# Decoder block on one core: where the down projection's operands are split, and the order of the passes in a granule

## The chip, the cores and the metric

The kernel runs on one core of a Trainium2 chip. The metric is the device time of one execution in microseconds. Three runs of the kernel before took 2098.62, 2100.62 and 2102.5 us (median 2100.62).

## The reference

One decoder block over 512 tokens of width 2048, everything in float32: a token mixer (gated linear attention and differential attention beside each other, from one input projection, joined by one output projection) and a gated MLP with a causal convolution of width 3, each between two RMS norms and added to the residual. Nearly all arithmetic is in four matrix products; the change touches the last one most.

```python
h = rmsnorm(x, attn_pre_norm)
proj = h @ w_in                                   # 512 x 2048 by 2048 x columns of both groups
o = concat(gla(...proj...), diff_attention(...proj...))
x = x + rmsnorm(o @ w_o, attn_post_norm)

h = rmsnorm(x, ffn_pre_norm)
up = h @ w_ffn_in                                 # 2048 x 11264
a, b = up[..., :5632], up[..., 5632:]
a = conv_w[0]*a[t-2] + conv_w[1]*a[t-1] + conv_w[2]*a[t] + conv_b
f = (gelu(a) * b) @ w_ffn_out                     # 5632 x 2048
x = x + rmsnorm(f, ffn_post_norm)
```

## The kernel before

**Three passes for one product.** TensorE multiplies a rounded float32 form. A float32 operand is therefore cut into a high half (the rounded value, a copy on ScalarE) and a low half (the rest, a subtraction on VectorE), and a product is the sum of three passes: high by high, high by low, low by high. `split` (L149 to L151) does this for activations; `granule` (L137, L138) does it for a weight tile of 128 x 1024, called a granule. The halves of the weights lie in one tensor `ring` with three places for high and three for low halves; in the down stage every fourth granule goes to a pair of spare tiles, `xhi` and `xlo`. Activations lie in `ah` and `al`. So in a row of the profile `ring<-raw,ring` or `ring<-rt,ring` on DVE is the making of a low half, and `bank<-ring,ah` is a pass on either half of the weights.

**Stages.** The projections are computed by a scheme of Winograd's kind: each unit has seven segments (x0, z0, y0, z1, x1, y1, y2) in place of eight block products, of two granules each. The right-hand blocks are sums of weight blocks (made by VectorE, L1212 and L1230, or by loads from the POOL queue that add to the tile in SBUF, L1195 and L1455), the left-hand ones are sums of token blocks, called a11, s5, s2, s3, a12, s7 and a22. In the profiled execution the stages lie about so: start and first projections to 130 us; the mixer's input projection with both attentions woven in to 620; output projection and the way to the MLP, with the first 512 columns of the MLP (`first_pair`, two calls) by plain products, to 880; twenty units of the up projection (ten groups of 512 columns, two branches) to about 1640; ten units of the down projection (five chunks, two halves of the columns) to 2045; the columns of `first_pair` through the down projection (`last_group`, `ffn_out_part`) and the last norm to the end.

**The passes.** `mm_n` (L191 to L193), `InUnit.run` (L742 to L748), `down_prods` (L1349 to L1351) and `ffn_out_part` (L1553 to L1555) issue the three passes of each 128 rows next to each other: high by high, then the one on the weights' low half and the one on the activations' low half. `up_prods` (L1247 to L1249) and `mm_t` (L173 to L175) do so too. A scheduler orders the instructions of each engine within its rules; the change-over from up to down units (`change_over`, `run_in_order`) is in an order written out by hand, with small jobs hung on granules by `at`.

**The down projection's operands.** After the second branch of a group, `product` makes the activations u0 and u1 and `token_sums` stores a11, a12, a22 and, after four sums of 128 x 512 by VectorE (L1322), s5, s2, s7 and s3 to DRAM, 256 KB each, in tensors `sd{c}{name}` (two groups make a chunk c; seven stores a group). The sums use two buffers, tag "sum", in turn. In the down stage `prepare` loads 512 KB of an operand into a tile `st` and splits it: ScalarE writes `ah` (L150), VectorE writes `al` (L151), 35 times in all. In the change-over five of these are cut into a load and a split, hung on different granules, and the last group's four sums are hung on four granules. `first_pair` stores its activations in `ud0`, which the last stage loads and splits in the same way, twice.

## Time and profile before

| | |
|---|---|
| runs, median | 2100.62 us |
| profiled execution | 2097.49 us |
| its span | 2095.8 us |
| split of a weight granule: ScalarE, VectorE | 1.06 us, 1.22 us |
| sum of 128 x 512 on VectorE (L1322) | 0.68 us |
| operand loads `st<-sd..`, 512 KB | 35, median 3.2 to 8.2 us to landing, by tensor |
| operand stores `sd..<-u` and `sd..<-s`, 256 KB | 70, median 2.1 to 6.5 us to landing, by tensor |

The profile is of one execution, on the hardware's own clock. The span runs from the first to the last recorded instruction; the execution took 1.7 us more than that. PE is TensorE's matmuls, PEld its weight loads, DVE VectorE, ACT ScalarE, POOL GpSimd, SP the engine that issues most loads and stores. Matmuls are pipelined: their recorded durations overlap, and the spacing of their starts tells the pace. In a list of waits, "bank L1350 <- DVE ring L138" means that the matmul at L1350 stood until VectorE's instruction at L138 had ended. In a row of the timeline the bracket gives the idle time of the engine before the instruction and what ended it.

### The profile page before, as it was taken

The page shows a single profiled execution, that of the slowest core. Times are in us where ns is not written, and L with a number is a line of the kernel's source. Part 1 is how long each engine was busy: PE and PEld are TensorE (multiplying, and loading weights), DVE is VectorE, ACT ScalarE, POOL GpSimd, SP SyncE. Part 2 cuts the span into 40 slices and gives each one's busy share as a digit, 9 for nine tenths or more (in the row PEclk, how much of TensorE's full clock was granted, in tenths as well). Part 3 has the DMA queues.
Part 4 walks back from the last instruction along what each step waited for, and adds up shares of the span by engine and source line. Part 5 has one row for each costly group of instructions (what it writes and reads, how often), then busy time and mean ns, then how long its engine had stood idle before and what let it go on. Part 6 is the DMA issues. An engine that isn't in the chain of part 4 may idle for free.

```text
span 2095.8 us, 35570 instructions
## 1 busy us (share of the span) xinstructions
PE 2059.0 (98%) x14449; PEld 1900.7 (91%) x14449; DVE 1509.7 (72%) x1802; ACT 1002.5 (48%) x1306; POOL 286.3 (14%) x306
## 2 busy tenths in 40 slices
PE   7999999999999999999999999999999999999997
PEld 6699999999988889899999999999999878787786
DVE  5967777676762255976777777777777778888877
ACT  5544444455742233454554554555455554444443
POOL 0112222322200000011011111110111110110100
PEclk9999999999999999999999999999999999999999
DMA  5488887878884344447667577667766876776763
GB/s 210 121 186 182 193 193 177 180 176 196 197 229 151 96 159 151 138 107 192 153 150 192 144 162 186 142 160 173 167 157 181 240 211 166 189 195 159 175 166 141
DMA packets 280696, 358.60 MB, mean 171 GB/s; under 512 B 14592, under 2 KB 221876, under 8 KB 278612
## 3 DMA queue, kind: packets, MB, share of 16 engines
q1 hardware_dynamic: 191380, 259.85, 37.2%
q0 software_dynamic: 84800, 94.38, 29.7%
q8 instruction: 113, 1.85, 0.4%
q10 hardware_dynamic: 4352, 2.10, 0.3%
q14 instruction: 51, 0.42, 0.1%
HBM read 311.72 MB, written 44.56 MB: 170 GB/s over the span
## 4 chain that ended last, share of the span: by engine, by line
PE 60%; issue 30%; DMA 3%; DVE 3%; POOL 3%; ACT 1%; SPq 0%; POOLq 0%; DVEq 0%; ACTq 0%
PE bank L1247 6%; PE bank L1248 6%; PE bank L1249 6%; PE bank L192 3%; PE bank L193 3%; PE bank L191 3%; PE bank L742 3%; PE bank L744 3%; PE bank L743 3%; PE bank L746 3%; PE bank L748 3%; PE bank L747 3%; PE bank L173 2%; PE bank L175 2%; PE bank L174 2%
## 5 line engine op out<-in xcount | busy, mean ns | idle before, releaser
L138 DVE TENSOR_TENSOR ring<-raw,ring 128x1024 fp32r<-128x1024 f32 x315 | 383.4, 1222 | 281.0 <-ACT ring L137 271.1
L137 ACT ACTIVATE ring<-raw 128x1024 fp32r<-128x1024 f32 x315 | 333.2, 1060 | 509.2 <-PE bank L1248 113.9
L1247 PE MATMUL bank<-ah,ring 128*128 128x256 f32 x1280 | 353.4, 276 | 0.0
L1248 PE MATMUL bank<-al,ring 128*128 128x256 f32 x1280 | 353.4, 276 | 0.0
L1249 PE MATMUL bank<-ah,ring 128*128 128x256 f32 x1280 | 353.4, 276 | 0.0
L137 ACT ACTIVATE ring<-rt 128x1024 fp32r<-128x1024 f32 x221 | 233.4, 1060 | 247.8 <-PE bank L1248 154.9
L138 DVE TENSOR_TENSOR ring<-rt,ring 128x1024 fp32r<-128x1024 f32 x221 | 269.1, 1221 | 86.9 <-ACT ring L137 86.7
L1247 PEld LDWEIGHTS bank<-ah,ring 128*128 128x128 f32 x1280 | 240.3, 188 | 0.1
L1248 PEld LDWEIGHTS bank<-al,ring 128*128 128x128 f32 x1280 | 240.3, 188 | 0.1
L1249 PEld LDWEIGHTS bank<-ah,ring 128*128 128x128 f32 x1280 | 240.3, 188 | 0.0
L1350 PE MATMUL bank<-ring,ah 128*128 128x512 f32 x424 | 166.2, 392 | 6.3 <-DVE ring L138 6.3
L1351 PE MATMUL bank<-ring,al 128*128 128x512 f32 x424 | 165.1, 389 | 0.0
L1349 PE MATMUL bank<-ring,ah 128*128 128x512 f32 x424 | 158.3, 391 | 0.0
L192 PE MATMUL bank<-ring,ah 128*128 128x512 f32 x280 | 110.0, 394 | 0.6 <-DVE ring L138 0.6
L191 PE MATMUL bank<-ring,ah 128*128 128x512 f32 x280 | 109.6, 397 | 0.0
L193 PE MATMUL bank<-ring,al 128*128 128x512 f32 x280 | 109.3, 393 | 0.0
L1195 POOL DMA_DIRECT2D raw<-in_w_ffn_in_dram x40 | 51.2, 1309 | 395.5 <-DVE ring L138 395.5
L1350 PEld LDWEIGHTS bank<-ring,ah 128*128 128x128 f32 x424 | 79.6, 188 | 26.1 <-DVE ring L138 9.9
L1349 PEld LDWEIGHTS bank<-ring,ah 128*128 128x128 f32 x424 | 79.5, 188 | 18.1 <-ACT ring L137 1.4
L1195 POOL DMA_DIRECT2D rt<-in_w_ffn_in_dram x40 | 50.9, 1271 | 326.9 <-DVE ring L138 292.4
L1351 PEld LDWEIGHTS bank<-ring,al 128*128 128x128 f32 x424 | 79.6, 188 | 16.3
L746 PE MATMUL bank<-ring,ah 128*128 128x256 f32 x320 | 92.7, 290 | 1.7 <-ACT ring L137 1.0
(346 smaller groups left out, 5670.9 us busy)
## 6 DMA issues: line engine op xcount, KB each, us to landing
raw<-in_w_ffn_in_dram SPq DMA_DIRECT2D x96, 512.0 KB, 5.0
raw<-in_w_in_dram SPq DMA_DIRECT2D x56, 512.0 KB, 4.8
raw<-in_w_ffn_out_dram SPq DMA_DIRECT2D x48, 512.0 KB, 6.2
raw<-in_w_in_dram POOLq DMA_DIRECT2D x40, 512.0 KB, 7.1
rt<-in_w_ffn_in_dram SPq DMA_DIRECT2D x40, 512.0 KB, 5.6
rt<-in_w_ffn_in_dram POOLq DMA_DIRECT2D x40, 512.0 KB, 6.1
raw<-in_w_ffn_in_dram POOLq DMA_DIRECT2D x40, 512.0 KB, 6.8
raw<-in_w_o_dram SPq DMA_DIRECT2D x32, 512.0 KB, 3.9
```

Of the source, the lines that this page charges most:

```text
L137: act(hi, raw, AF.Copy)
L138: tt(lo, raw, hi.bitcast(F32), ALU.subtract)
L191: mm(banks[t], ah[:, t, s, :], w[0][:, k, :], start=st, stop=False)
L192: mm(banks[t], ah[:, t, s, :], w[1][:, k, :], start=False, stop=False)
L193: mm(banks[t], al[:, t, s, :], w[0][:, k, :], start=False, stop=sp)
L746: mm(o, sh[:, n, kk, :], wh[:, k, :], start=st, stop=False, **NOW)
L1247: mm(o, wh, sh[:, :, kk, :], start=start and kk == 0 and n == 0, stop=False, **NOW)
L1248: mm(o, wh, sl[:, :, kk, :], start=False, stop=False, **NOW)
L1249: mm(o, wl, sh[:, :, kk, :], start=False, stop=kk == HK - 1, **NOW)
L1349: mm(b[j], sh[:, o:o + P], w[0][:, q, :], start=start and st == 0, stop=False, **NOW)
L1350: mm(b[j], sh[:, o:o + P], w[1][:, q, :], start=False, stop=False, **NOW)
L1351: mm(b[j], sl[:, o:o + P], w[0][:, q, :], start=False, stop=st == 3, **NOW)
```

## The change

Two things change, and the number of matmuls does not.

First, the operands of the down projection are split where they are made. `store_split` has ScalarE write the high half into a small tile and VectorE write the low half in place, and stores both, 256 KB each, into two tensors (`h` and `l`). `token_sums` now gives eleven jobs: four sums and seven `store_split`s. Sums and high halves share one tag, "t2", of four buffers; s7 is made in the place of a21. `prepare` becomes two loads of 512 KB straight into `al` and `ah`. In the change-over the five loads are hung on other granules, their splits are gone, and the last group's eleven jobs are hung on eleven granules. `first_pair` stores its two parts split as well.

Second, in `mm_n`, `InUnit.run`, `down_prods` and `ffn_out_part` all passes on the weights' high half come first and those on the low half last. `up_prods` and `mm_t` stay.

```diff
     def mm_n(banks, t, g, w, slots=tuple(range(KT))):
-        for k in range(2):
+        for v, p, k in ((ah, 0, 0), (al, 0, 0), (ah, 0, 1), (al, 0, 1), (ah, 1, 0), (ah, 1, 1)):
             i = 2 * g + k
-            st, sp, s = i == 0, i == KT - 1, slots[i]
-            mm(banks[t], ah[:, t, s, :], w[0][:, k, :], start=st, stop=False)
-            mm(banks[t], ah[:, t, s, :], w[1][:, k, :], start=False, stop=False)
-            mm(banks[t], al[:, t, s, :], w[0][:, k, :], start=False, stop=sp)
+            mm(banks[t], v[:, t, slots[i], :], w[p][:, k, :], start=i == 0 and p == 0 and v is ah,
+               stop=i == KT - 1 and p == 1)
...
+                for w in (wh, wl):
+                    for n in range(2):
...
+                                mm(o, sh[:, n, kk, :], w[:, k, :], start=st, stop=sp_, **NOW)
+                                if w is wh:
+                                    mm(o, sl[:, n, kk, :], w[:, k, :], start=False, stop=False, **NOW)
...
+    def half_tile(name, dt=F32):
+        return fp.tile([P, 2, 256], dt, name=name, tag="t2", bufs=4)
...
+    def store_split(dst, src, hi):
+        split(hi, src.bitcast(F32R), src)
+        dma(dst(0), hi.bitcast(F32))
+        dma(dst(1), src)
...
-        dma(ud0[:, 2 * pr:2 * pr + 2, :], c)
+        store_split(lambda v: ud0[v][:, 2 * pr:2 * pr + 2, :], c, small_tile("hi", F32R).rearrange("p (n t) -> p n t", n=2))
...
-        def put(n, src):
-            dma(sd[c][n][:, i, :].rearrange("p (n t) -> p n t", n=2), src)
-
-        def add(n, x, y, op):
+        def add(n, x, y, op, dst=None):
             def go():
-                t = made[n] = fp.tile([P, 2, 256], F32, name=n, tag="sum", bufs=2)
-                tt(t, made.get(x, x) if isinstance(x, str) else x, y, op)
-                put(n, t)
+                made[n] = half_tile(n) if dst is None else dst
+                tt(made[n], made.get(x, x) if isinstance(x, str) else x, y, op)
             return go
 
-        put("a11", a11)
-        put("a12", a12)
-        put("a22", a22)
-        return (add("s5", a21, a22, ALU.subtract), add("s2", "s5", a11, ALU.subtract),
-                add("s7", a11, a21, ALU.subtract), add("s3", "s2", a12, ALU.add))
+        def out(n, src=None):
+            def go():
+                store_split(lambda v: sd[c][n][v][:, i, :].rearrange("p (n t) -> p n t", n=2),
+                            made[n] if src is None else src, half_tile("hi", F32R))
+            return go
+
+        return (add("s5", a21, a22, ALU.subtract), add("s7", a11, a21, ALU.subtract, a21),
+                add("s2", "s5", a11, ALU.subtract), out("s5"), add("s3", "s2", a12, ALU.add), out("s2"),
+                out("s3"), out("a11", a11), out("s7"), out("a12", a12), out("a22", a22))
...
     def prepare(c, n):
-        raw = small_tile("st")
-        dma(raw, sd[c][n].rearrange("p g x -> p (g x)"))
-        split(piece(ah, *place[n]), piece(al, *place[n]), raw)
+        for v, d in zip((ah, al), sd[c][n]):
+            dma(piece(v, *place[n]).bitcast(F32), d.rearrange("p g x -> p (g x)"))
 
     def down_prods(b, op, g, w, start):
         sh, sl = (piece(v, *place[op]) for v in (ah, al))
-        for j in range(2):
-            for q in range(2):
-                o = 512 * g + 256 * q + P * j
-                st = 2 * g + q
-                mm(b[j], sh[:, o:o + P], w[0][:, q, :], start=start and st == 0, stop=False, **NOW)
-                mm(b[j], sh[:, o:o + P], w[1][:, q, :], start=False, stop=False, **NOW)
-                mm(b[j], sl[:, o:o + P], w[0][:, q, :], start=False, stop=st == 3, **NOW)
+        for p in range(2):
+            for j in range(2):
+                for q in range(2):
+                    o = 512 * g + 256 * q + P * j
+                    st = 2 * g + q
+                    mm(b[j], sh[:, o:o + P], w[p][:, q, :], start=start and st == 0 and p == 0,
+                       stop=st == 3 and p == 1, **NOW)
+                    if p == 0:
+                        mm(b[j], sl[:, o:o + P], w[0][:, q, :], start=False, stop=False, **NOW)
...
-        prepare_at(0, "s2", (u, "x1", 0), (u, "y1", 0))
-        prepare_at(0, "s3", (u, "x1", 1), (d0, "x0", 0))
-        prepare_at(0, "s7", (u, "y1", 1), (u, "y2", 0))
-        prepare_at(0, "a12", (d0, "x0", 0), (d0, "z0", 0))
-        prepare_at(0, "a22", (u, "y2", 0), (d0, "y0", 0))
+        at(u, "x1", 1, lambda: prepare(0, "s2"))
+        at(u, "x1", 1, lambda: prepare(0, "s3"))
+        at(u, "y1", 1, lambda: prepare(0, "s7"))
+        at(u, "y1", 1, lambda: prepare(0, "a12"))
+        at(u, "y2", 1, lambda: prepare(0, "a22"))
...
-        for where in ((d0, "z0", 0), (d0, "y0", 0), (d0, "z1", 0), (d0, "x1", 0)):
+        spread = [(d0, seg, g) for seg in ("z0", "y0", "z1", "x1", "y1") for g in range(2)] + [(d1, "x0", 0)]
+        for where in spread:
             at(*where, lambda: late_sums.pop(0)())
...
+        for v, p, k in [(v, 0, k) for k in range(4) for v in range(2)] + [(0, 1, k) for k in range(4)]:
+            mm(b, us[k][v][:, tk], gr[k // 2][p][:, k % 2, :], start=(v, p, k) == (0, 0, 0),
+               stop=(p, k) == (1, 3))
```

What stands on the engines now, at three places (numbers behind a name tell buffers apart).

PE in a down unit, one granule into two banks; of the passes on `ring,ah` before the change, L1349 is on the high half of the weights and L1350 on the low half. Before (each bank's first L1349 stands a few rows ahead of these):

```order
L1350 MATMUL bank_17768<-ring_84,ah_79 128x512
L1351 MATMUL bank_17768<-ring_84,al_80 128x512
L1349 MATMUL bank_17768<-ring_84,ah_79 128x512
L1350 MATMUL bank_17768<-ring_84,ah_79 128x512
L1351 MATMUL bank_17768<-ring_84,al_80 128x512
L1350 MATMUL bank_17769<-ring_84,ah_79 128x512
L1351 MATMUL bank_17769<-ring_84,al_80 128x512
L1349 MATMUL bank_17769<-ring_84,ah_79 128x512
L1350 MATMUL bank_17769<-ring_84,ah_79 128x512
L1351 MATMUL bank_17769<-ring_84,al_80 128x512
```

After, where L1357 is the pass on `ah` with either half, and the rows with x2 at the end of each granule are on the low half:

```order
L1357 MATMUL bank_17548<-ring_84,ah_79 128x512
L1360 MATMUL bank_17548<-ring_84,al_80 128x512
L1357 MATMUL bank_17548<-ring_84,ah_79 128x512
L1360 MATMUL bank_17548<-ring_84,al_80 128x512
L1357 MATMUL bank_17549<-ring_84,ah_79 128x512
L1360 MATMUL bank_17549<-ring_84,al_80 128x512
L1357 MATMUL bank_17549<-ring_84,ah_79 128x512
L1360 MATMUL bank_17549<-ring_84,al_80 128x512
L1357 MATMUL bank_17548<-ring_84,ah_79 128x512 x2
L1357 MATMUL bank_17549<-ring_84,ah_79 128x512 x2
```

Eight passes on the high half stand ahead of the four on the low half, where one on each half alternated.

VectorE in the up stage, after the product of the first group (`u_9365` and `u_9192` before, `u_9180` and `u_9235` after, hold its activations; L1230 and L1239 add weight blocks; L138 makes low halves of weights). Before:

```order
L1322 TENSOR_TENSOR s5_9539<-u_9365,u_9192 128x512
L138 TENSOR_TENSOR ring_84<-rt_9425,ring_84 128x1024
L1322 TENSOR_TENSOR s2_9542<-s5_9539,u_9365 128x512
L138 TENSOR_TENSOR ring_84<-raw_9608,ring_84 128x1024
L1230 TENSOR_TENSOR rt_9425<-rt_9425,raw_9724 128x1024
L1322 TENSOR_TENSOR s7_9545<-u_9365 128x512
L138 TENSOR_TENSOR ring_84<-raw_9610,ring_84 128x1024
L138 TENSOR_TENSOR ring_84<-raw_9722,ring_84 128x1024
L1322 TENSOR_TENSOR s3_9548<-s2_9542,u_9192 128x512
L138 TENSOR_TENSOR ring_84<-raw_9724,ring_84 128x1024
L1275 TENSOR_TENSOR u_9606<-bank_9553,u_9606 128x2x256
```

After, with the four sums at L1327 and the low halves of the operands at L151; first from the sum s5 on:

```order
L1327 TENSOR_TENSOR s5_9578<-u_9180,u_9235 128x512
L138 TENSOR_TENSOR ring_84<-rt_9467,ring_84 128x1024
L1327 TENSOR_TENSOR u_9180<-u_9180 128x2x256
L1327 TENSOR_TENSOR s2_9581<-s5_9578,u_9180 128x512
L138 TENSOR_TENSOR ring_84<-raw_9677,ring_84 128x1024
L1239 TENSOR_TENSOR rt_9467<-rt_9467,raw_9793 128x1024
L151 TENSOR_TENSOR s5_9578<-s5_9578,hi_9583 128x512
L1327 TENSOR_TENSOR s3_9588<-s2_9581,u_9235 128x512
L138 TENSOR_TENSOR ring_84<-raw_9679,ring_84 128x1024
L138 TENSOR_TENSOR ring_84<-raw_9791,ring_84 128x1024
```

and from there to the last of the seven splits:

```order
L151 TENSOR_TENSOR s2_9581<-s2_9581,hi_9590 128x512
L151 TENSOR_TENSOR s3_9588<-s3_9588,hi_9595 128x512
L138 TENSOR_TENSOR ring_84<-raw_9793,ring_84 128x1024
L151 TENSOR_TENSOR u_9180<-u_9180,hi_9600 128x2x256
L1284 TENSOR_TENSOR u_9675<-bank_9622,u_9675 128x2x256
L138 TENSOR_TENSOR ring_84<-raw_9677,ring_84 128x1024
L151 TENSOR_TENSOR u_9180<-u_9180,hi_9605 128x2x256
L138 TENSOR_TENSOR ring_84<-raw_9679,ring_84 128x1024
L151 TENSOR_TENSOR u_9235<-u_9235,hi_9610 128x2x256
L151 TENSOR_TENSOR u_9235<-u_9235,hi_9615 128x2x256
```

The four sums stand close together, and seven splits of half size have come in among the low halves of the weights.

ScalarE at the same place, after the change; each `hi` is a tile of tag "t2":

```order
L150 ACTIVATE hi_9583<-s5_9578 128x512
L137 ACTIVATE ring_84<-raw_9679 128x1024
L137 ACTIVATE ring_84<-raw_9791 128x1024
L150 ACTIVATE hi_9590<-s2_9581 128x512
L1282 ACTIVATE u_9675<-bank_9469 128x2x256
L150 ACTIVATE hi_9595<-s3_9588 128x512
L137 ACTIVATE ring_84<-raw_9793 128x1024
L150 ACTIVATE hi_9600<-u_9180 128x512
L137 ACTIVATE ring_84<-raw_9677 128x1024
L150 ACTIVATE hi_9605<-u_9180 128x512
L137 ACTIVATE ring_84<-raw_9679 128x1024
L150 ACTIVATE hi_9610<-u_9235 128x512
```

Before, the rows between L1271 and the next L1085 were weight splits and one L1273 alone.

SyncE, which issues loads and stores in this order, where the second chunk's operands are loaded. Before:

```order
L48 DMA st_17404<-sd1a11_8335 128x1024
L48 DMA st_17440<-sd1s5_8338 128x1024
L48 DMA sd4s2_8360<-s2_17090 128x512
L48 DMA sd4s7_8361<-s7_17120 128x512
L48 DMA st_17480<-sd1s2_8339 128x1024
L102 DMA raw_17300<-in_w_ffn_out_dram 128x2x512
L102 DMA raw_17302<-in_w_ffn_out_dram 128x2x512
L102 DMA raw_17368<-in_w_ffn_out_dram 128x2x512
L102 DMA raw_17370<-in_w_ffn_out_dram 128x2x512
L48 DMA sd4s3_8362<-s3_17160 128x512
```

After:

```order
L48 DMA al_80<-sd1s5l_8350 128x1024
L48 DMA ah_79<-sd1s5h_8349 128x1024
L102 DMA raw_17824<-in_w_ffn_out_dram 128x2x512
L48 DMA al_80<-sd1s2l_8352 128x1024
L48 DMA ah_79<-sd1s2h_8351 128x1024
L102 DMA raw_17826<-in_w_ffn_out_dram 128x2x512
L102 DMA raw_17896<-in_w_ffn_out_dram 128x2x512
L48 DMA al_80<-sd1s3l_8356 128x1024
L48 DMA ah_79<-sd1s3h_8355 128x1024
L102 DMA raw_17898<-in_w_ffn_out_dram 128x2x512
L48 DMA al_80<-sd1a12l_8346 128x1024
L48 DMA ah_79<-sd1a12h_8345 128x1024
```

An operand was one row (`st`) and is now two, `al` and `ah`.

66 lines of the change are left out of this document (22 added, 44 removed).

## The prediction

> **What bounds the kernel now.** I read the page first: the engines' shares, the slices, the chain that ended last.
>
> ```profile
> PE 2059.0 (98%) x14449; PEld 1900.7 (91%) x14449; DVE 1509.7 (72%) x1802; ACT 1002.5 (48%) x1306; POOL 286.3 (14%) x306
> ...
> PE   7999999999999999999999999999999999999997
> ...
> PE 60%; issue 30%; DMA 3%; DVE 3%; POOL 3%; ACT 1%; SPq 0%; POOLq 0%; DVEq 0%; ACTq 0%
> ```
>
> PE sets the time: it is busy in every slice but the two ends, and the chain is PE and its issue. The change leaves the number of matmuls alone, so it can only fill PE's gaps or open new ones. Where the gaps lie comes from the windows (columns: stretch and length, then busy us and instructions of PE, PEld, DVE, ACT, POOL; then PE clock, DMA share, GB/s).
>
> ```profile
> 130.00:620.00 490.00, 484.63 (x3934) 470.58 (x3933) 344.68 (x576) 257.20 (x426) 109.90 (x124) 1.00 0.83 189
> ...
> 850.00:900.00 50.00, 50.00 (x287) 43.92 (x286) 46.38 (x44) 23.41 (x26) 2.57 (x2) 1.00 0.34 85
> 880.00:1630.00 750.00, 750.00 (x6596) 749.11 (x6595) 563.97 (x554) 385.18 (x438) 100.77 (x79) 1.00 0.69 162
> 1630.00:1700.00 70.00, 67.35 (x364) 56.64 (x363) 53.20 (x53) 35.74 (x41) 7.15 (x6) 1.00 0.84 245
> 1700.00:2045.00 345.00, 339.68 (x1487) 277.89 (x1486) 286.65 (x306) 157.43 (x160) 40.19 (x34) 1.00 0.68 176
> 1750.00:1800.00 50.00, 50.00 (x222) 41.44 (x221) 41.27 (x46) 23.74 (x24) 5.33 (x6) 1.00 0.74 194
> 1800.00:1850.00 50.00, 48.47 (x213) 39.50 (x212) 40.43 (x44) 19.77 (x20) 6.49 (x6) 1.00 0.76 183
> ```
>
> The up stage (880 to 1630) has no gap at all; the stretch 1800 to 1850 has nine matmuls fewer than its neighbour, whose 222 in 50 us give the undisturbed spacing, 0.225 us for 512 columns. (In the up stage 6596 in 750 us give 0.114 us for 256 columns.) So the down stage and the hand-ordered change-over ahead of it lose time, the up stage does not. What PE waits for there comes from its list of waits (waited for: us in total, times, longest).
>
> ```profile
> PE bank L158 <- DVE xt L247: 10.4, 2, 9.5
> PE bank L1350 <- DVE ring L138: 6.3, 8, 1.0
> PE bank L1350 <- DVE xlo L138: 1.6, 3, 0.8
> ...
> PE bank L746 <- ACT ring L137: 1.0, 1, 1.0
> PE bank L175 <- DVE xlo L138: 0.8, 1, 0.8
> PE bank L1554 <- DVE xlo L138: 0.8, 1, 0.8
> PE bank L748 <- DVE ring L138: 0.8, 1, 0.8
> ...
> PE bank L192 <- DVE ring L138: 0.6, 1, 0.6
> ```
>
> Every wait of the down stage is at L1350, the matmul on the weights' low half, and is for DVE's L138, which makes that half. The first row (start) and L746 (high half) are not touched. The costliest of the L1350 waits, PE first, then DVE ahead of it, then ACT:
>
> ```profile
> 1820.59 0.62 PE L1349 MATMUL bank<-ring,ah 128*128 128x512 f32 x2
> 1822.24 0.50 PE L1350 MATMUL bank<-ring,ah 128*128 128x512 f32 x1 [1.03 <-DVE ring L138]
> ```
>
> ```profile
> 1818.70 1.22 DVE L1230 TENSOR_TENSOR rt<-rt,raw 128x1024 f32<-128x1024 f32 x1
> 1819.84 1.22 DVE L151 TENSOR_TENSOR al<-st,ah 128x1024 fp32r<-128x1024 f32 x1
> 1820.97 1.22 DVE L138 TENSOR_TENSOR ring<-rt,ring 128x1024 fp32r<-128x1024 f32 x1
> ```
>
> ```profile
> 1812.88 1.06 ACT L137 ACTIVATE xhi<-rt 128x1024 fp32r<-128x1024 f32 x1 [4.60 <-DMA rt<-in_w_ffn_out_dram]
> ```
>
> An accumulating load landed late, ACT had stood for 4.60 us, DVE worked off the backlog, and the operand's own split (L151) stood right in front of the low half that PE needed. Both parts of the change act here.
>
> **Gain: the late low halves.** Two matmuls began at 1820.59, the second some 0.23 us later, at 1820.82; the next at 1822.24. That is 1.42 us for a spacing of 0.23, so the wait cost 1.19 where the record says 1.03: 0.16 more, the drained pipe. The 11 waits of L1350 (6.3 + 1.6 = 7.9 us) then cost 7.9 + 11 x 0.16 = 9.7 us; L1554, L748 and L192, one each, (0.8 + 0.8 + 0.6) + 3 x 0.16 = 2.7 us. L175 is in a function that the change leaves as it is. Together 12.4 us can go.
>
> Do they go? With the passes reordered, eight matmuls of a down granule lie ahead of the first one on the low half, where one or two did: six more at least, 6 x 0.225 = 1.35 us. The longest wait, 1.19, is inside that. L748 gets 14 to 15 more of 0.114 (1.6 us), L1554 as much as L1350, L192 three of 0.225 (0.7 us, for a wait of 0.76). The 35 splits that leave the down stage come on top. Their rows, and those of what replaces them (columns: busy us, mean ns):
>
> ```profile
> L151 DVE TENSOR_TENSOR al<-st,ah 128x1024 fp32r<-128x1024 f32 x35 | 42.6, 1217 | 0.0
> ...
> L150 ACT ACTIVATE ah<-st 128x1024 fp32r<-128x1024 f32 x34 | 35.8, 1052 | 9.7 <-PE bank L1350 8.6 <-DMA st<-ud 0.9
> ```
>
> ```profile
> L137 ACT ACTIVATE ring<-rt 128x1024 fp32r<-128x1024 f32 x157 | 167.0, 1064 | 182.2 <-PE bank L1248 150.8 <-issue 9.4 <-DMA raw<-in_w_ffn_in_dram 6.6
> ...
> L1271 ACT ACTIVATE u<-bank 128x512 f32<-128x512 f32 x20 | 11.6, 580 | 0.0
> ```
>
> ```profile
> L1322 DVE TENSOR_TENSOR s<-s,u x20: 683/688/694, 973.2 to 1679.7; 128x512 f32<-128x512 f32 x20
> ```
>
> 42.6 us leave DVE (busy 286.65 of 345 there) and 35.8 leave ACT. As neither is the bound on average, this saves nothing beyond the same waits.
>
> **Cost 1: the splits in the up stage.** Each of ten groups gets seven half-size splits: 7 x 0.69 = 4.8 us of DVE and 7 x 0.58 = 4.1 us of ACT; nine groups lie in the up stage. DVE has room there on average (563.97 of 750), but in the rows of the new order the group fills DVE: from the first sum to the last half-size split stand seven low halves and one weight add (8 x 1.22), four sums, seven splits and one addition of a bank (12 x 0.69), 18 us while PE goes through seven granules, 19 us. A granule has slack: 24 matmuls of 0.114 are 2.7 us; with three ring slots a slot falls free two granules (5.4 us) before PE needs its new contents, of which ACT's 1.06 and DVE's 1.22 use 2.3. So 3.1 us of delay are hidden at each granule. What could use them up are the stores: the new split writes into one of four small tiles, and a tile is free only once its store has landed. Before, DVE waited so:
>
> ```profile
> DVE s L1322 <- DMA sd1s<-s: 6.1, 2, 3.7
> ```
>
> ```profile
> DMA to landing us min/median/max: 2.0/4.8/5.9
> ```
>
> (The second row is for the eight stores of tile sd1s.) The reuses form chains of three links (a tile is written by ACT, stored, written again), with about two weight splits, 5.4 us of PE's time, in a link. A split and a store of the median length, 0.58 + 4.8, just fit. Bounds: 0, or 2.5 us for each of nine groups, 22 us, if the delays add up; I take 1.5 us in all, near the lower end, because before the change a wait of 3.7 us on DVE cost PE nothing in this stage.
>
> **Cost 2: the first pairs.** Two full-size splits, 2 x 1.22 us of DVE, join the stretch 850 to 900, where DVE has 46.38 of 50 us. It can't hide all: 0 to 2.5 us, taken 1.5.
>
> **Cost 3: the change-over.** Five split steps leave it, seven half-size ones with fourteen stores come in, in a stretch with a DMA share of 0.84. It loses 2.65 us now (70.00 - 67.35). I let 2.0 us of that stand or come back; bounds 0 and 5.
>
> **Cost 4: the traffic.** An operand now arrives as two halves of the full size.
>
> ```profile
> q1 hardware_dynamic: 191380, 259.85, 37.2%
> q0 software_dynamic: 84800, 94.38, 29.7%
> ...
> rt<-in_w_ffn_out_dram POOLq DMA_DIRECT2D x20, 512.0 KB, 8.5
> ...
> sd1a<-u SPq DMA_DIRECT2D x6, 256.0 KB, 6.5
> ```
>
> The hardware queue moved 259.85 MB in 0.372 x 2095.8 = 780 us of 16 engines, 3.0 us each MB. 35 more loads of 0.52 MB are 18.4 MB, 55 us over some 400 us of down stage: its share goes from 0.68 to about 0.82. The loads sit on SP's queue among the weights, in units with an even number, where they may push an accumulating load (8.5 us already) later. Bounds: 0, or 1.2 us in each of five such units, 6 us; taken 1.0, since the new lead of 1.35 us takes most of it.
>
> **Sum.** -12.4 + 1.5 + 1.5 + 2.0 + 1.0 = -6.4 us. The profiled execution took 2097.49 us (its span 2095.8, 1.7 around it), which becomes 2091.1; the median of the runs shown is 2100.62, 3.1 above that execution. On the median's scale the forecast is 2100.6 - 6.4 = **2094.2 us**.
>
> **A rule of the skill against the change.** The row of sd1a stands for three stores issued close together: 6.5 us each, where a lone 256 KB store took 2.0. The Trainium skill, DMA: Bandwidth & Descriptors, "Rules for kernel authors", says to coalesce small transfers into large ones and to aim at 1 MiB; the change does the reverse, with two stores of 256 KB where one was. That rule would have the bunch of fourteen decide: it is the first rival below. The same page, "Queues, rings and completion order", says that an engine takes turns between queues packet by packet; by that a store beside one accumulating load would take about twice its 2.0 us, 4 us, and the first rival would not come to pass. The measured median of 4.8 and maximum of 5.9 lie between the two, nearer the first.
>
> **Rivals.**
>
> 1. *ACT waits for stores in the up stage (slower).* A link with a store of sd1a's length takes 0.58 + 6.5 = 7.1 us instead of 5.4; three links put ACT 5.1 us behind, 2.0 more than the hidden 3.1. It decides from a landing time of 5.9 us (3 x 1.07 = 3.2). With the scatter of the landing times that is 1 to 2.5 us each for nine groups: 9 to 22 us in place of 1.5. Time 2094.2 + 7.5 to 2094.2 + 20.5, 2102 to 2115. For it: the rows of sd1a and sd1s, and a DMA share of 0.69. Against it: PE lost nothing to DVE's 3.7 us. Chance 0.19.
>
> 2. *The traffic gives the gain back (no change).* Costs 3 and 4 at their upper ends, 5 + 6 us instead of 3: 2094.2 + 8 = 2102, or half of that, 2098. For it: accumulating loads start every such stall (the 4.60 us above). Against it: those waits are short beside the lead. Chance 0.24.
>
> 3. *All of it is covered.* The gain stays whole and the costs are 0 to 3: 2088 to 2091. For it: neither DVE nor ACT is full on average. Chance 0.13.
>
> That the scheduler undoes the reordering is excluded by the rows of the new order: the low half comes last.
>
> **How the numbers follow.** The forecast (2091.5 to 2098) has 0.44. This kernel's measurement can tell about 0.2%, 4.2 us: faster means under 2096.4. Of the forecast's chance 0.40 lies there, with 0.13 of the third and 0.02 of the second rival: 0.55. Slower means above 2104.8: 0.14 of the first rival and 0.04 of the second, 0.18. The rest, 0.27, is within. The range, 2086 to 2109, leaves out the upper half of the first rival and, below, a gain larger than all that I can find.
>
> **What would show it.** Right: no wait of PE for DVE's L138 in the down stage, 222 matmuls in nearly every 50 us of it, and 750 of 750 us busy in the up stage. Cost 1 shows as waits of PE in the up stage, with ACT's high-half splits waiting for a DMA on the sd tiles; cost 2 as a gap at about 900; costs 3 and 4 as waits at the high half in the down stage, for ACT behind a DMA. The forecast is wrong if waits at the high half replace those at the low half one for one, or if the interleaving of the mixer, where the reordered passes move other work too (PE lacks 490 - 484.63 = 5.4 us there now), comes out differently by several us.

## The result, and the profile after

The changed kernel takes 2149.96 us (median of four runs, 2147.87 to 2154.86), against 2099.73 us before: ratio 1.0237, 95% interval 1.0215 to 1.0258, **slower by 50 us**. Its profiled execution took 2154.86 us with a span of 2153.1 us. The page, as before: busy time, PE by slices, the chain.

```profile
PE 2080.7 (97%) x14449; PEld 1915.7 (89%) x14449; DVE 1508.8 (70%) x1837; ACT 1000.7 (46%) x1341; POOL 281.3 (13%) x306
...
PE   7999999999989999999999999999999999999998
...
issue 42%; PE 22%; DMA 4%; POOL 4%; DVE 1%; ACT 1%; POOLq 0%; ACTq 0%; DVEq 0%
```

The same 14449 matmuls have spread over 57 us more (2153.1 - 2095.8). That is 7 us more than the medians say, because the changed kernel's profiled execution was the longest of its four; figures from one execution, here and below, are sure to some 5 us at best. PE is still busy in nearly all slices, so the page hides where. Four landmarks of the trace show it: the first matmul of the up units, the first and the last of the down units, and the end of the span. (us; each number is the difference of two start times in the trace.)

| | start to first up | up stretch | down stretch | rest | span |
|---|---|---|---|---|---|
| before | 885.2 | 756.2 | 401.8 | 52.6 | 2095.8 |
| after | 894.9 | 804.3 | 403.9 | 50.0 | 2153.1 |
| difference | +9.7 | +48.1 | +2.1 | -2.6 | +57.3 |

PE's list of waits after, the rows that are new or answer to those of before:

```profile
PE bank L1258 <- DVE ring L138: 22.6, 33, 1.1
...
PE bank L1256 <- ACT ring L137: 5.6, 5, 3.5
PE bank L833 <- DVE p L821: 5.2, 1, 5.2
PE bank L1357 <- ACT ring L137: 4.8, 6, 2.0
PE bank L1357 <- issue: 3.1, 2, 1.6
...
PE bank L1357 <- ACT xhi L137: 1.8, 1, 1.8
```

No matmul of the down units (L1357) waits for a low half any more. Some wait for a high half instead, 4.8 + 1.8 = 6.6 us, and 3.1 us more stand under "issue", where the profile shows nothing that was waited for: 9.7 us in all, against 7.9. And the up units (L1256, L1258), which never waited, have 38 waits of 28.2 us in all, most at the low half. The reader can follow one group. ScalarE first:

```profile
993.57 0.63 ACT L150 ACTIVATE hi<-s 128x512 fp32r<-128x512 f32 x1 [3.04 <-DMA sd0s5l<-s]
...
999.84 0.63 ACT L150 ACTIVATE hi<-u 128x512 fp32r<-128x512 f32 x1 [3.21 <-DMA sd0s3h<-hi]
...
1013.58 1.06 ACT L137 ACTIVATE ring<-rt 128x1024 fp32r<-128x1024 f32 x1 [2.32 <-DMA rt<-in_w_ffn_in_dram]
...
1017.87 2.01 ACT L137 ACTIVATE ring<-rt 128x1024 fp32r<-128x1024 f32 x2 [2.70 <-DMA rt<-in_w_ffn_in_dram]
```

Then PE:

```profile
1020.24 0.39 PE L1258 MATMUL bank<-s5h,ring 128*128 128x256 f32 x1 [0.58 <-DVE ring L138]
```

```profile
1027.01 0.38 PE L1258 MATMUL bank<-s2h,ring 128*128 128x256 f32 x1 [1.05 <-DVE ring L138]
```

Two kinds of waits stand on ScalarE: for stores that have to free a tile (as the first rival had it), and some 15 us later for adding loads (`rt`) that land late. The two longest waits of PE in this group come behind the second kind. Over the up stretch, ScalarE's waits for those loads were, before and after:

```profile
ACT ring L137 <- DMA rt<-in_w_ffn_in_dram: 6.3, 4, 2.5
```

```profile
ACT ring L137 <- DMA rt<-in_w_ffn_in_dram: 68.5, 24, 6.0
```

The adding loads themselves take longer to land, before (first row) and after (the last column is the median in us):

```profile
rt<-in_w_ffn_in_dram POOLq DMA_DIRECT2D x38, 512.0 KB, 6.1
rt<-in_w_ffn_in_dram POOLq DMA_DIRECT2D x39, 512.0 KB, 7.5
```

So which is it: the tiles, the work of the splits, or the bytes? And which part of the change cost the 9.7 us ahead of the up units? That is what the experiments ask.

### The profile page after: what moved, and what is told of

Same layout as the page of the kernel before. It is cut to its first block, busy times and chain, and to the rows that moved or that the text cites. A ratio compares the mean times of both kernels' runs of the same rounds, so it can differ in the third digit from the quotient of the medians.

```text
span 2153.1 us, 35924 instructions
## 1 busy us (share of the span) xinstructions
PE 2080.7 (97%) x14449; PEld 1915.7 (89%) x14449; DVE 1508.8 (70%) x1837; ACT 1000.7 (46%) x1341; POOL 281.3 (13%) x306
## 4 chain that ended last, share of the span: by engine, by line
issue 42%; PE 22%; DMA 4%; POOL 4%; DVE 1%; ACT 1%; POOLq 0%; ACTq 0%; DVEq 0%
PE bank L190 8%; PE bank L1357 6%; PE bank L1360 3%; POOL rt L1204 2%; PE bank L1544 2%; POOL raw L1204 1%; DMA rt<-in_w_ffn_out_dram 1%; PE bank L175 1%; DMA raw<-in_w_ffn_out_dram 1%; PE bank L173 1%; PE bank L174 1%; DMA raw<-in_w_in_dram 1%; DMA dstd<-dst 0%; DVE ring L138 0%; ACT ring L137 0%
## 5 line engine op out<-in xcount | busy, mean ns | idle before, releaser
L138 DVE TENSOR_TENSOR ring<-raw,ring 128x1024 fp32r<-128x1024 f32 x315 | 382.8, 1221 | 272.5 <-ACT ring L137 271.6
L137 ACT ACTIVATE ring<-raw 128x1024 fp32r<-128x1024 f32 x315 | 332.7, 1058 | 468.0 <-PE bank L190 91.4
L138 DVE TENSOR_TENSOR ring<-rt,ring 128x1024 fp32r<-128x1024 f32 x221 | 267.9, 1220 | 141.1 <-ACT ring L137 141.0
L1258 PE MATMUL bank<-ah,ring 128*128 128x256 f32 x1280 | 356.1, 278 | 6.4 <-DVE ring L138 6.4
L137 ACT ACTIVATE ring<-rt 128x1024 fp32r<-128x1024 f32 x221 | 230.7, 1057 | 278.4 <-PE bank L1257 97.6
L1256 PE MATMUL bank<-ah,ring 128*128 128x256 f32 x1280 | 354.0, 277 | 0.0
L1357 PE MATMUL bank<-ring,ah 128*128 128x512 f32 x848 | 269.2, 390 | 7.9 <-ACT ring L137 4.8
L1258 PEld LDWEIGHTS bank<-ah,ring 128*128 128x128 f32 x1280 | 240.3, 188 | 10.0 <-DVE ring L138 9.2
L1256 PEld LDWEIGHTS bank<-ah,ring 128*128 128x128 f32 x1280 | 240.3, 188 | 0.6 <-ACT ring L137 0.2
L1357 PEld LDWEIGHTS bank<-ring,ah 128*128 128x128 f32 x848 | 159.1, 188 | 44.4 <-ACT ring L137 7.1
L190 PE MATMUL bank<-ring,ah 128*128 128x512 f32 x560 | 177.6, 395 | 0.2 <-ACT ah L150 0.2
L190 PEld LDWEIGHTS bank<-ring,ah 128*128 128x128 f32 x560 | 106.4, 190 | 22.7 <-ACT ah L150 0.6
L746 PE MATMUL bank<-ring,ah 128*128 128x256 f32 x640 | 117.8, 282 | 0.6 <-ACT ring L137 0.6
L742 PE MATMUL bank<-ah,ring 128*128 128x256 f32 x640 | 117.6, 282 | 0.0
L746 PEld LDWEIGHTS bank<-ring,ah 128*128 128x128 f32 x640 | 99.3, 189 | 1.4 <-ACT ring L137 0.8
L1258 PE MATMUL bank<-s5h,ring 128*128 128x256 f32 x320 | 91.8, 287 | 8.4 <-DVE ring L138 8.4
L742 PEld LDWEIGHTS bank<-ah,ring 128*128 128x128 f32 x640 | 99.3, 188 | 0.1
```

The source lines that it names most:

```text
L137: act(hi, raw, AF.Copy)
L138: tt(lo, raw, hi.bitcast(F32), ALU.subtract)
L190: mm(banks[t], v[:, t, slots[i], :], w[p][:, k, :], start=i == 0 and p == 0 and v is ah, stop=i == KT - 1 and p == 1)
L742: mm(o2, cw, sh[:, :, kk, :], start=st, stop=sp_, **NOW)
L746: mm(o, sh[:, n, kk, :], w[:, k, :], start=st, stop=sp_, **NOW)
L1256: mm(o, wh, sh[:, :, kk, :], start=start and kk == 0 and n == 0, stop=False, **NOW)
```

## The experiments

In the expectations the mixer is the time from 130 us to the last matmul of its units (612.9 us before, 624.2 after). All landmarks first, from the profiled execution of each kernel (us); the texts below refer to this table. The boundary between "down" and "rest" shifts with the order of the passes: 20 of the last group's matmuls start ahead of the last down matmul in e1_passes and e3_down_passes, where before there were 12, so the sum of the two columns is the safer figure. The ratio is to the kernel before, with its interval.

| run | first up | up | down | rest | ratio |
|---|---|---|---|---|---|
| before | 885.2 | 756.2 | 401.8 | 52.6 | |
| changed kernel | 894.9 | 804.3 | 403.9 | 50.0 | 1.0237 (1.0215 to 1.0258) |
| e1_passes | 896.3 | 756.2 | 404.4 | 49.9 | 1.0032 (1.0020 to 1.0044) |
| e2_split | 886.0 | 795.2 | 406.9 | 52.7 | 1.0198 (1.0181 to 1.0215) |
| e3_down_passes | 885.0 | 757.2 | 403.2 | 50.2 | 0.9991 (0.9982 to 1.0000) |
| e5_spread | 895.0 | 790.2 | 400.9 | 49.6 | 1.0187 (1.0169 to 1.0206) |
| e6_twice | 885.7 | 767.6 | 405.5 | 52.5 | 1.0067 (1.0044 to 1.0091) |
| e8_hi_only | 894.8 | 760.4 | 401.0 | 50.1 | 1.0054 (1.0038 to 1.0069) |
| e4_t2_6 | 896.2 | 799.2 | 401.3 | 49.9 | 1.0205 (1.0179 to 1.0232) |
| e7_no_inunit | 887.1 | 756.2 | 403.2 | 50.4 | 0.9991 (0.9982 to 1.0001) |
| e9_late | 896.0 | 771.5 | 400.2 | 49.6 | 1.0104 (1.0081 to 1.0127) |
| e11_hi_load | 894.5 | 761.5 | 396.4 | 49.5 | 1.0042 (1.0031 to 1.0053) |
| e10_inunit_level | 903.7 | 756.2 | 405.6 | 52.8 | 1.0082 (1.0055 to 1.0108) |
| e12_last | 885.6 | 756.2 | 400.4 | 52.6 | 0.9999 (0.9988 to 1.0010) |

### The two halves of the change apart

**e1_passes**: the changed kernel's `mm_n`, `InUnit.run`, `down_prods` and `ffn_out_part` in the kernel before.

```diff
 def down_prods(b, op, g, w, start):
...
-        for j in range(2):
-            for q in range(2):
...
+        for p in range(2):
+            for j in range(2):
+                for q in range(2):
...
```

> All four reordered passes, operands split in the down stage as before. Theory A (the loss is the operands' splitting and storing in the up stage, some 48 us between the first up and the first down matmul): that stretch returns to 756 us, the down stage loses its low-half waits (about 10 us), the mixer keeps what the changed kernel shows there (its 494 us against 483): total about 2098 us, 2093 to 2103. Theory B (the order of the passes is what costs): the up stretch stays near 800 us and the total above 2140 us.

**e2_split**: the changed kernel with those four functions as before.

> Operands split where they are made, passes in the order of before. Theory A: the up stretch takes about 804 us as in the changed kernel, the mixer 483; the low-half waits of the down stage stay in part: total 2140 to 2158 us. Theory B: up stretch 756 us, total 2095 to 2105 us.

e1_passes has the up stretch of before to the tenth, and the whole loss ahead of it; e2_split has most of the loss in the up stretch and next to none ahead of it. So the two losses belong to the two halves: splitting and storing costs 39 us in the up stretch (795.2 - 756.2; 48 together with the new passes, and where the other 9 come from was not followed), the new passes cost 11 us in the mixer (896.3 - 885.2). Theory B falls. e2_split took 2142.49 us, inside theory A's range. The total of e1_passes, 2107.59 us, is above the expected 2103: the down stretch did not get its 10 us back.

**e3_down_passes**: the kernel before with `down_prods` and `ffn_out_part` alone in the new order.

> The kernel before with the passes reordered in the down units and the last group alone. Theory A: no wait for the low half in the down stage, 10 to 11 us less than before: 2088 to 2092 us, mixer 483 us. Rival (late loads then stop the matmuls at the high half instead): within 3 us of before, 2097 to 2103 us, with waits at the high half of 8 us or more.

Measured: 2099.16 us, ratio 0.9991, and the down stretch is 1.4 us longer than before (with the rest, 453.4 us against 454.4). The rival holds in its time; of its "waits at the high half of 8 us or more" about half came, as follows. PE's waits in the down stage:

```profile
PE bank L1350 <- DVE acc L1359: 5.0, 3, 3.0
PE bank L1350 <- ACT ring L137: 3.9, 3, 2.3
```

All 11 waits for the low half are gone; in their place stand six others that sum to 8.9 us, 5.0 for VectorE to empty a bank (L1359) and 3.9 for the high half. The three for the high half stand behind late loads: ScalarE's copy had waited 11.42, 2.92 and 3.93 us for one. The longest of the others (3.0), followed back: ScalarE stood behind an operand's load, and VectorE's addition behind the splits that this held up.

```profile
1960.59 1.06 ACT L150 ACTIVATE ah<-st 128x1024 fp32r<-128x1024 f32 x1 [5.14 <-DMA st<-ud]
```

```profile
1961.69 1.22 DVE L151 TENSOR_TENSOR al<-st,ah 128x1024 fp32r<-128x1024 f32 x1 [3.04 <-ACT ah L150]
1962.83 1.22 DVE L138 TENSOR_TENSOR ring<-rt,ring 128x1024 fp32r<-128x1024 f32 x1
1963.97 1.27 DVE L1359 TENSOR_TENSOR acc<-acc,bank 128x512 f32<-128x512 f32 x2
```

### What the up stretch waits for

**e5_spread**: ScalarE's splits held back behind later weight splits (a scheduling edge, no wait): one or two jobs at most segments and four at the last.

```diff
-                    if gi < NG - 1:
-                        for f in sums:
-                            f()
+                    late_sums.extend(sums)
...
+    def some(n):
+        for _ in range(min(n, len(late_sums))):
+            with tc.issue_after(made_hi[0].ins):
+                late_sums.pop(0)()
```

> The changed kernel, with a group's seven split-and-store jobs of the up stage held back so that they stand on ScalarE over some 30 us in place of 16. Theory A1 (the bunch decides: tiles waiting for stores, stores crowding the adding loads): the up stretch falls from 804 to 760 to 780 us, total 2105 to 2128 us. Theory A2 (the added bytes themselves decide, wherever they stand): up stretch above 790 us, total above 2135 us.

790.2 us and 2138.51 in all: by its numbers A2, though 14 us better than the changed kernel. ScalarE's waits for stores fell by half, those for the rt loads nearly stayed (61.7 us, 22 times). It didn't decide the matter: the jobs were spread, but over the same busy stretch of the DMA engines, as e9_late shows below.

**e6_twice**: the kernel before with each operand block stored a second time.

```diff
         def put(n, src):
             dma(sd[c][n][:, i, :].rearrange("p (n t) -> p n t", n=2), src)
+            dma(sd2[c][n][:, i, :].rearrange("p (n t) -> p n t", n=2), src)
```

> The kernel before, but each operand block of the up stage is stored twice (the second time into a tensor that nobody reads): the changed kernel's bytes and fourteen stores a group, with no half-size split on ScalarE or VectorE and no new load. Theory bytes (the stores crowd the adding loads): the up stretch, 756 us before, goes up by 20 us or more, with ScalarE waiting for rt loads. Theory engines (the splits on VectorE and ScalarE and their tiles decide): up stretch 756 to 764 us, total within 8 us of before.

**e8_hi_only**: the changed kernel without the stores of the low halves.

```diff
         dma(dst(0), hi.bitcast(F32))
-        dma(dst(1), src)
...
-        for v, d in zip((ah, al), sd[c][n]):
+        for v, d in zip((ah, al), (sd[c][n][0],) * 2):
```

> The changed kernel without the store of the low halves; the high half is loaded in the place of the low one too, so the low parts of the operands are left out of the result. All splits remain, the stores of the up stage are those of before (seven of 256 KB a group), the loads of the down stage are the changed kernel's. Theory bytes: up stretch back to 756 to 768 us. Theory engines: up stretch 785 us or more.

The work of the splits alone costs 4.2 us (760.4 - 756.2; theory bytes), the stores alone 11.4 us (767.6 - 756.2; between the theories), both together 48.1. So neither holds by itself: taking the seven low stores away removes 44 of the 48 us, yet the same number of stores and bytes beside an unchanged VectorE and ScalarE costs a quarter of that. e6_twice differs from the changed kernel in two things, and does not tell them apart. It lacks the splits: its second store goes out with the first, where in the changed kernel the low half is stored only when VectorE has made it, and the adding loads, for which POOL waits until VectorE has read a tile, may go out later themselves. And its stores stand elsewhere: those of one group go out from 1112 to 1140 us, six of them ahead of the sums, and an idle stretch of the DMA engines (1124 to 1127) lies among them; in the changed kernel all fourteen go out from 1147.6 to 1168.5 us, in one busy stretch (share 0.93 from 1148 to 1184).

**e4_t2_6**: more buffers for the tiles that wait for stores.

```diff
-        return fp.tile([P, GR], dt, name=name, tag="t4", bufs=6)
+        return fp.tile([P, GR], dt, name=name, tag="t4", bufs=5)
...
-        return fp.tile([P, 2, 256], dt, name=name, tag="t2", bufs=4)
+        return fp.tile([P, 2, 256], dt, name=name, tag="t2", bufs=6)
```

> The changed kernel with six buffers of tag t2 in place of four (and five small tiles in place of six). Theory tiles (a high half waits for a store to free its tile, and the weight splits behind it on ScalarE come late): ScalarE's waits for stores, 61 us in the changed kernel, fall below 25 us, and the up stretch from 804 to below 780 us. Theory bytes: waits for stores fall, the up stretch stays above 790 us since the rt loads still land late.

ScalarE's groups (busy us, mean ns, then idle before and its releasers), first the changed kernel, then e4_t2_6:

```profile
L150 ACT ACTIVATE hi<-u 128x512 fp32r<-128x512 f32 (+1 forms) x37 | 22.5, 630 | 29.5 <-DMA sd1s3h<-hi 7.5 <-DMA sd2s3h<-hi 6.8 <-DMA sd3s3h<-hi 6.8
L150 ACT ACTIVATE hi<-s 128x512 fp32r<-128x512 f32 x27 | 16.9, 626 | 31.3 <-DMA sd0s5l<-s 7.3 <-DMA sd1s5l<-s 7.1 <-DMA sd3s5l<-s 6.5
```

```profile
L150 ACT ACTIVATE hi<-u 128x512 fp32r<-128x512 f32 (+1 forms) x37 | 22.6, 633 | 24.8 <-DMA sd3s5l<-s 5.8 <-DMA sd1s5l<-s 5.6 <-DMA sd2s5l<-s 5.0
...
L150 ACT ACTIVATE hi<-s 128x512 fp32r<-128x512 f32 x27 | 17.0, 630 | 3.3 <-DVE s L1327 2.8
```

ScalarE's idle time ahead of these copies, nearly all of it waits for tiles, fell from 60.8 to 28.1 us (a little less than expected), and the up stretch from 804.3 to 799.2 only, a difference that two executions can show by chance; the waits for rt loads stayed at 65.6 us. The chain of tiles, on which the first rival was priced, is therefore not what costs most: half of it gone won 5 us. (That the small tiles are one fewer could hide a gain; nothing in the run waits for them.)

**e9_late**: the splits and stores of a11, s7, a12 and a22, eight of the fourteen stores, moved again, now into the stretch of each unit in which the DMA engines stand idle. The kernel before shows that stretch (the column before the last is the DMA share):

```profile
1156.00:1168.00 12.00, 12.00 (x108) 12.00 (x108) 11.14 (x12) 8.55 (x11) 0.00 (x0) 1.00 0.01 3
1132.00:1156.00 24.00, 24.00 (x214) 24.00 (x213) 16.28 (x18) 11.87 (x14) 3.39 (x3) 1.00 1.00 234
```

```diff
         u.y2()
+        turned = ups.index(u) % 2
+        some(4 if turned else 2)
         nxt.z0()
+        some(3 if turned else 2)
```

> The changed kernel with all its splits, bytes and stores, but the splits and stores of a11, s7, a12 and a22 of a group held back on ScalarE by four to six granules more, into the some 12 us of each unit of the up stage in which the DMA engines stand idle (before the change: DMA share 0.00 to 0.03 from 1156 to 1168 us). Theory place (the stores cost only because they are queued ahead of and among the adding loads of the busy stretch): up stretch from 804 down to 756 to 770 us, total 2100 to 2116 us. Theory volume (so many stores cost it wherever they stand): up stretch above 785 us.

771.5 us: 33 of the 48 us are gone with every split, byte and store still there (1.5 us short of what was expected). ScalarE's waits for rt loads are 36.0 us, 15 times, and PE's at the low half 7.5 us, 14 times. In the group at 1140 us the eight stores go out from 1167.9 to 1176.0 us, 25 to 33 us after the group's first store, where in the changed kernel it was 13 to 21. So the place of these splits and stores decides two thirds of the loss. The two moved together; that the stores are the larger part follows from e8_hi_only, where all the splits in their old place, with half the stores, cost 4.2 us. The six stores of s5, s2 and s3, which stayed in the busy stretch, are the likely rest, which was not tried.

The runs together tell tiles from loads. ScalarE's idle time ahead of the `hi` copies is 28.1 us in e4_t2_6, 31.0 in e5_spread and 33.5 in e9_late, nearly the same, while the up stretch is 799.2, 790.2 and 771.5 us. It goes, nearly in step, with ScalarE's waits for rt loads (us):

| | before | e8_hi_only | e9_late | e6_twice | e2_split | e5_spread | e4_t2_6 | changed |
|---|---|---|---|---|---|---|---|---|
| waits for rt loads | 6.3 | 26.6 | 36.0 | 41.4 | 55.8 | 61.7 | 65.6 | 68.5 |
| up stretch | 756.2 | 760.4 | 771.5 | 767.6 | 795.2 | 790.2 | 799.2 | 804.3 |

### The down stretch

**e11_hi_load**: as e8_hi_only, and the low halves are not loaded either.

```diff
-        for v, d in zip((ah, al), (sd[c][n][0],) * 2):
+        for v, d in zip((ah,), (sd[c][n][0],)):
```

> As the run that stores the high halves only, and now the down stage loads them only: the operand loads of the down stage are those of before in bytes (35 of 512 KB), without any split; the low parts of the operands are stale and so left out of the result. Theory traffic (the doubled operand loads give the gain of the down stage back): from the last up matmul to the last down matmul 380 to 385 us, against 390 with both halves loaded. Rival (the weights' own adding loads set the waits, whatever the operands bring): 388 us or more.

From the last up matmul to the last down matmul it takes 385.5 us, against 390.1 in e8_hi_only: between the two bounds, nearer the first. The windows of the two down stretches, e11_hi_load first:

```profile
1656.00:2052.40 396.40, 393.05 (x1750) 325.55 (x1749) 301.40 (x321) 163.18 (x168) 46.59 (x40) 1.00 0.71 193
```

```profile
1655.20:2056.10 400.90, 393.46 (x1749) 323.60 (x1748) 297.64 (x320) 158.58 (x168) 46.49 (x40) 1.00 0.81 236
```

In these two executions the doubled loads (DMA share 0.81 in place of 0.71) cost 4.6 us. By the medians, 2111.46 and 2108.67, it is 2.8 us, and the intervals of the two ratios overlap, so the size is not sure. Down stretch and rest together were 454.4 us before; they are 451.1 with the doubled loads and 445.9 with half of them. So with the splits gone, the passes reordered and the low halves neither stored nor loaded, the gain that was forecast nearly appears (8.5 us), and the doubled loads take 5 of it back; the changed kernel, which also stores the low halves in the change-over, has 453.9.

### The mixer

**e7_no_inunit**: the new order everywhere but in `InUnit.run`.

> The kernel before with the passes reordered everywhere but in the mixer's units. If the mixer's loss (483 to 494 us) comes from the order within its units: mixer 481 to 484 us, total 2095 to 2100 us. If it comes from the rest (the first projections and the output projection): mixer 490 us or more, total above 2104 us.

First up at 887.1 us in place of 896.3: 9.2 of the 11.1 us belong to the order within the mixer's units. (The mixer takes 614.8 - 130 = 484.8 us, 0.8 above the bound.) Two things were found in it. One is a wait near the mixer's end, 5.1 us where before the last 20 us of the mixer had three of 2.4 us in all; PE in e1_passes, and ScalarE, which stood behind a load while VectorE's L821 needed its L820:

```profile
PE bank L833 <- DVE p L821: 5.1, 1, 5.1
```

```profile
612.69 0.63 ACT L150 ACTIVATE ah<-dt 128x512 fp32r<-128x512 f32 x1 [3.25 <-DMA dt<-dstd]
613.22 0.61 ACT L820 ACTIVATE p<-p 128x512 f32<-128x512 f32 x1
```

The other has no wait in it. In the same 100 us, with PE busy all the time, before and e1_passes:

```profile
130.00:230.00 100.00, 100.00 (x851) 99.24 (x850) 71.97 (x115) 49.42 (x68) 22.58 (x22) 1.00 0.82 181
```

```profile
130.00:230.00 100.00, 100.00 (x836) 99.05 (x835) 71.51 (x113) 48.72 (x67) 21.46 (x22) 1.00 0.81 180
```

Fifteen matmuls fewer, though eight of them are short ones of 64 columns of another product, which start later there. By the start times the median spacing of the units' matmuls (256 columns) went from 0.114 to 0.117 us. The median overstates the loss, since in both kernels the spacings lie mostly at 0.113 and at 0.118: the mean, without waits and half clock, went from 0.1183 to 0.1194 us, some 4 us over 3360 matmuls.

**e10_inunit_level**: the new order in `InUnit.run` alone, with both halves of a granule at offset 0 of their places in the ring.

```diff
-                place_w[0] = APART if self.turned else APART_N
+                place_w[0] = LEVEL
```

> The kernel before with the passes reordered in the mixer's units alone, and there with the two halves of a granule at offset 0 in the ring in place of the offsets apart that the kernel has for these units. Theory order (the place of the halves in memory does not matter with the new order, and the loss is the scheduler's new interleaving): median spacing of the units' matmuls 0.117 us as with all passes reordered, mixer 490 to 496 us. Theory place in memory: the spacing moves away from 0.117 by 0.003 us or more, in either direction, and the mixer with it by 5 us or more.

The median spacing goes to 0.120 us (mean 0.1227) and the first up matmul to 903.7 us, 7.4 later than in e1_passes. In the same window:

```profile
130.00:230.00 100.00, 100.00 (x820) 99.19 (x819) 69.69 (x108) 48.27 (x66) 20.52 (x21) 1.00 0.79 178
```

So with the new order the place of the halves in memory changes the spacing. Whether other offsets would give 0.114 with the new order was not tried, nor offset 0 with the old order: how much of the step from 0.114 to 0.117 is the place and how much the order of the passes stays open, as does what in the memory makes the difference.

### The new order in the last group alone

**e12_last**: the new order in `ffn_out_part` alone.

> The kernel before with the passes reordered in the last group alone, the one place where every run with the new order was shorter (from the last down matmul to the last of the group 39.7 to 40.0 us against 42.5). If that is a gain of its own: that stretch 39.7 to 40.2 us, everything ahead of it as before, total 2 to 3 us below the kernel before (ratio 0.9986 to 0.9991). Rival (it only moves a wait from the down units' end into the last group or back): no difference, ratio 0.9995 to 1.0005.

2099.63 against 2100.04 us, ratio 0.9999: no difference; the rival holds. The rest after the last down matmul is 52.6 us as before. The order in `ffn_out_part` is therefore not what makes the last column 2 to 3 us smaller in other rows; in every one of these `down_prods` has the new order too, and the boundary shifts as said above the table. No version here beats the kernel before.

## Why the prediction was wrong

The forecast was 2094.2 us in a range of 2086 to 2109; measured are 2149.96. By its steps:

- **Gain, 12.4 us.** The count was right: all 11 waits at the low half went in e3_down_passes, at once. The step that failed is "The longest wait, 1.19, is inside that" lead of 1.35 us. It took the waits as single events that a lead absorbs. With the low half out of the way, PE stood at the high half and at the emptying of banks, 8.9 us in place of 7.9 (recorded waits). Four of these six waits, 6.9 us, lead back to loads that landed late; that the other two do, and that it is the same lateness as before, is argued. Gain of the new order in the down stretch and the rest: 1.0 us. "As neither is the bound on average, this saves nothing beyond the same waits" failed too: the gain nearly came in e11_hi_load (8.5 us), where the splits have left the down stage and no loads were added.
- **Cost 1, the up stage: 1.5 us taken, bounds 0 and 22; measured 48.1.** The step that failed is the upper bound, and below it the reason for the lower end ("a wait of 3.7 us on DVE cost PE nothing"). The price looked at ScalarE's tiles. e4_t2_6 shows that halving those waits is worth 5 us; what was left out is that the stores and the adding loads use the same DMA engines in the same 24 us of each unit, where their share was 1.00 before. I had used the mean share of the stage, 0.69. The traffic was priced in the down stage alone, as Cost 4. The rows of before showed it: the row of sd1a was read as three stores issued close together, but two went out 0.4 us apart (1110.4 and 1110.8 us) and the third 13 us later. Single stores took as long where the DMA engines were busy: 5.2 and 6.1 us for those of 976.8 and 982.8 us (share 0.98 and 1.04 while they were under way), against 2.0 us for that of 1048.3 (share 0.37).
- **The first rival** had the right place and sign, with chance 0.19, but its mechanism was the tiles and its price 9 to 22 us. The rule of the Trainium skill that stood beside it (DMA: Bandwidth & Descriptors, "Rules for kernel authors": few large transfers) pointed the right way. It does not price the case by itself: seven stores more cost 11.4 us in the kernel before (e6_twice), the same seven taken out of the changed kernel win 44 (e8_hi_only), and eight moved, with none taken out, win 33 (e9_late).
- **Cost 2, the first pairs: 1.5 us taken.** The stretch from the mixer's last matmul to first up is 272.3 us in e2_split as it was before, so the splits cost nothing there. At 909.8 us in the changed kernel PE waits 0.5 us (0.7 with the drained pipe) for VectorE, which 10 us earlier had made one of the two splits (L151, 899.4); before there was no wait. That they belong together is argued. At most 0.7 us, then: below the 1.5, inside the bounds.
- **Cost 3, the change-over: 2.0 us taken.** In the 70 us around the first down matmul PE waits 2.7 us after (three times for L137, the high half), 2.65 before: the loss came back in another place, about as large as taken. The wait of 3.50 us at 1667 us, ahead of this stretch, is not in the term.
- **Cost 4, the traffic: 1.0 us taken.** e8_hi_only against e11_hi_load gives 4.6 us for the doubled loads by the profiles, 2.8 by the medians; the term was mis-sized but inside its bounds, and the DMA share went to 0.81 as worked out (0.82).
- **The mixer, +11 us**, a term that the sum did not have, was named as something that could make the forecast wrong, without a price or a chance: the rows of the new order were compared there only for what moved, not for where the operands lie.

The up stretch's 48.1 us can be added up from the trace: 28.2 us of recorded waits, 38 x 0.16 = 6.1 for the drained pipe, and the rest, some 14 us, in spacings that are long without a wait: by the start times 5 us at half clock (10 us at 0.50, from 1507 on and as below), 4 us in the matmul behind each wait, which takes 0.22 us in place of 0.11, and 5 us scattered. That the delay of VectorE and that of the loads feed each other, through the tiles that POOL's loads wait for, fits e6_twice and e8_hi_only (11.4 and 4.2 alone, 48.1 together), but no run isolates it, and the other place of the stores in e6_twice would fit as well.

## What to carry to other kernels

A wait that disappears from the list is a gain only if what was late is early now: follow it back to the load or queue that caused it, and ask where PE would meet that lateness next. Price added traffic where it is issued, by the DMA share of those microseconds and not of the stage; here stores next to loads that gate the next step were dear, and the same stores in an idle stretch far cheaper. A store's time to land, by where it was issued, shows such a stretch beforehand. When the order of matmuls changes, compare the spacing of their starts as well as the waits: the operands' offsets in memory may have to change with it, which was not shown here.

## What the runs showed of the hardware

The granted clock halves after less idling than I had thought. In the changed kernel a wait of 3.50 us, and 0.76 us soon after, were followed by 6.8 us at 0.50, the last 6 of which stand in these rows:

```profile
1668.00:1670.00 2.00, 0.00 (x0) 0.00 (x0) 0.00 (x0) 0.41 (x1) 0.00 (x0) 1.00 0.77 299
1670.00:1672.00 2.00, 0.54 (x3) 0.34 (x3) 1.28 (x2) 2.00 (x3) 0.00 (x0) 0.80 0.09 33
1672.00:1674.00 2.00, 2.00 (x9) 2.00 (x10) 2.00 (x2) 1.97 (x4) 0.00 (x0) 0.50 0.04 8
1674.00:1676.00 2.00, 2.00 (x12) 2.00 (x11) 2.00 (x4) 1.06 (x2) 0.00 (x0) 0.50 0.00 0
1676.00:1678.00 2.00, 2.00 (x11) 2.00 (x11) 2.00 (x4) 1.62 (x3) 0.00 (x0) 0.50 0.00 0
```

The kernel before has it too, at the mixer's end, where PE was busy 0.72 of 2 us and then 0.55 of 1:

```profile
598.00:600.00 2.00, 0.72 (x4) 0.32 (x3) 0.83 (x1) 1.92 (x3) 0.00 (x0) 1.00 0.04 14
600.00:601.00 1.00, 0.55 (x4) 0.55 (x5) 0.99 (x2) 0.57 (x2) 0.00 (x0) 0.92 0.00 0
601.00:602.00 1.00, 1.00 (x6) 1.00 (x6) 0.97 (x2) 0.24 (x1) 0.00 (x0) 0.50 0.27 41
602.00:603.00 1.00, 1.00 (x7) 1.00 (x6) 1.00 (x2) 1.00 (x2) 0.00 (x0) 0.50 0.91 274
```

Two waits, of 0.97 and 0.76 us, were enough here. The Trainium skill (TensorE: Matmul & The Clock Gate, "What's actually happening") has the clock halved after an idle window of some 3.4 us; the first place agrees with that, the second shows that a stretch which is only mostly idle can do it as well. It need not. In e4_t2_6 waits of 1.27 and 0.75 us, half a us between them, left the clock at 1.00 (first two rows); waits of 1.10 and 0.76 us, as close together, were followed by 0.50 (last three):

```profile
1181.00:1183.00 2.00, 0.73 (x5) 0.33 (x3) 0.52 (x1) 1.61 (x2) 0.00 (x0) 1.00 0.04 14
1183.00:1185.00 2.00, 1.25 (x11) 1.25 (x11) 1.97 (x3) 1.97 (x4) 0.00 (x0) 1.00 0.00 0
...
1503.00:1505.00 2.00, 0.90 (x8) 0.70 (x7) 0.13 (x1) 1.22 (x2) 0.00 (x0) 1.00 0.15 50
1505.00:1507.00 2.00, 1.24 (x7) 1.04 (x8) 1.97 (x2) 1.97 (x3) 0.00 (x0) 0.91 0.00 0
1507.00:1509.00 2.00, 2.00 (x11) 2.00 (x11) 1.97 (x3) 2.00 (x4) 0.00 (x0) 0.50 0.00 0
```

What decides between the two is not shown. In the kernel before the clock came back at 604.2 us: the 3.4 us at 0.50 lost 1.7 us, as much as the two waits together.
